# Jobs of the recurrence issued in three pieces, and a first stage whose modulation comes in four parts with other loads behind it

## The chip, the cores and the metric

The kernel runs on one core of one Trainium2 chip. The metric is the device time of one execution in microseconds (us). Five engines work side by side, each through its own list of instructions in order: PE (TensorE: matrix products and transposes), DVE (VectorE), ACT (ScalarE), POOL (GpSimd) and SP (SyncE, which here mostly issues transfers). In the profile, PE's weight loads stand under PEld. An instruction that depends on another engine waits for a semaphore, and everything behind it on its own engine waits with it.

## The reference

One layer for 512 noisy grid tokens and 128 context tokens (640 in all, width 1024):

```
sh1, sc1, g1, sh2, sc2, g2 = split(silu(cvec) @ w_ada + b_ada, 6)     # the modulation
h = rmsnorm(x, norm1_g) * (1 + sc1) + sh1
u_rw, u_na, gate_rw, gate_na = split(h @ w_in)
o_rw, state = rwkv(u_rw)           # forward and backward recurrence over time, 8 heads of 64
  # per step: sa = s @ a;  s = s * w + sa b^T + v k^T;  y = s @ r
  # bonus = sum(r * k_bonus * r_k) * v, added to the normalised y
o_na = neighbourhood or context attention (q, k normalised; v)
x = x + g1 * ((sigmoid(gate_rw) * (o_rw @ w_o_rwkv) + sigmoid(gate_na) * (o_na @ w_o_na)) @ w_out)
h2 = rmsnorm(x, norm2_g) * (1 + sc2) + sh2
x = x + g2 * ((silu(h2 @ ffn_w1) * (h2 @ ffn_w3)) @ ffn_w2)
```

The scan is computed in chunks, by a triangular inverse within each chunk.

## The kernel before, in words

**First stage (0 to 62 us).** Tokens stand in five blocks of 128 (four of the grid, one of context, loaded by `x_load`). `norm_x(i)` normalises a block and transposes it on PE (tile `xt`) into `xT`. The modulation's first two vectors are made in parts: `ada_part(k0, n, c0)` loads tiles `wa` of `w_ada` through SP and multiplies them with the conditioning vectors into `psa`, and `mod_part(k0, n, c0)` copies `psa` to `rows` (DVE), transposes `rows` on PE (`pc`), makes scale `A` and shift `B` on DVE, and then, for the n blocks of 128 columns of the width that begin at k0, makes `h` from `xT`: the high half on ACT, `ht` and the low half on DVE. Columns k0 = 0 and 1 are part one, 2 and 3 part two, 4 to 7 part three. The first user of `h` is the Q projection: `tok_gen` steps through four chunks of `w_qkv`, each loaded as `wst`, split into `whi` (ACT) and `wlo` (DVE), and multiplied in steps of three matmuls of 512 columns (`acc`): 40 steps, 120 matmuls, then K and V follow. The numbers in `qp` say how many steps of Q stand on PE behind each tile of `wa`. What SP loads for later stages (`win`, `upw`, `gup`, `f`) is put by the scheduler into its list where it fits.

**Recurrence (240 to 640 us).** It runs over four groups of heads (ct 0 to 3). For each, `inv` builds the inverse of a triangular matrix `RL` on DVE in 30 steps s of a product (`pr`) and a sum; on PE stand meanwhile independent matmuls of later or earlier projections, the fillers (`fl`, 128x320), whose number behind each step is written out in `plan`. Three jobs (`v_job`, `t_job`, `g_job`, on lines 8 to 15, 0 to 7 and so on of the chunk) are put into `inv` at the steps in `jobs`, (2, 9, 28) or (2, 8, 28): each of the second and third makes 192 records of 64x64 on PE in one go, 64 of `t_job` (L1274) and 128 of `g_job` (L1216, L1219, L1252 or L1263). The results' masks follow on DVE at the steps in `mds`. `bonus` sums over the heads with a constant matrix, in two halves: matmul (L1162), product on DVE (L1164), matmul, product, each at a step of its own; `g_job` reads the tile rows `R_`, `BK` and `vp`. After step 30 DVE transposes `RL` into `RT` (L1346), and PE goes on with the carry products from L1359 on.

In the first stage `manual_schedule` keeps PE's instructions in the written order; in the other engines' lists the scheduler places them. In the recurrence the generators of the stage and of the fillers are stepped by the tables, and that sets PE's and DVE's order.

## Time and profile before

| | us |
|---|---|
| median of 3 runs | 1145.75 (1142.03 to 1146.5) |
| profiled execution, its own time | 1141.53 |
| span of the profiled execution, first to last instruction | 1139.8 |
| PE busy in the span | 1106.1 |
| DVE busy | 781.1 |
| ACT busy | 533.7 |
| POOL busy | 193.7 |
| mean granted clock of PE | 0.997 |

PE is busy for 97% of the span, so an instruction that is moved there only matters through PE's idle time, some 34 us in all. The other engines are idle for much longer, and their idle time counts only where PE waits for them. The views below name, for a stretch or an engine, what it did and what ended its idle time; "issue" means that the engine waited for nothing the profile shows.

### The profile page before, as it was taken

How to read it: one execution, taken by the hardware profiler on the slowest of the kernel's cores; microseconds unless marked ns; L12 is line 12 of the kernel's file. 1: busy time of each engine (PE TensorE's matmuls, PEld its weight loads, DVE VectorE, ACT ScalarE, POOL GpSimd, SP SyncE). 2: the span in 40 equal slices, each digit the busy share in tenths (PEclk: the TensorE clock that was granted, in tenths of full speed). 3: DMA queues.
4: the chain of work that ended last, by engine and by line, in shares of the span. 5: the costliest groups of instructions: out<-in, count | busy, mean ns of one | idle time of the engine just before them, and what ended most of it. 6: DMA issues, size and time to landing. Idle time of an engine off the chain costs nothing.

```text
span 1139.8 us, 26864 instructions
## 1 busy us (share of the span) xinstructions
PE 1106.1 (97%) x11160; PEld 979.3 (86%) x11160; DVE 781.1 (69%) x1646; ACT 533.7 (47%) x1056; POOL 193.7 (17%) x261
## 2 busy tenths in 40 slices
PE   6999999999999999999899999999999999999998
PEld 4688878799888988888898788999899989998997
DVE  4565465769658948946777846996478647864776
ACT  4444566664574565566353525654134413441340
POOL 1163244320101211111100511200001010101000
PEclk9999999999999999999999999999999999999999
DMA  9752677654423443343734961223112321232122
GB/s 342 266 107 97 191 263 264 200 152 111 126 65 96 115 121 94 107 110 98 276 97 134 260 215 64 90 77 120 65 59 90 114 72 56 93 108 77 56 94 93
DMA packets 60482, 149.16 MB, mean 131 GB/s; under 512 B 7460, under 2 KB 22436, under 8 KB 60360
## 3 DMA queue, kind: packets, MB, share of 16 engines
q1 hardware_dynamic: 54312, 129.85, 35.0%
q0 software_dynamic: 4032, 14.68, 6.6%
q10 hardware_dynamic: 2016, 2.90, 0.8%
q8 instruction: 88, 1.44, 0.5%
q14 instruction: 34, 0.28, 0.1%
HBM read 118.41 MB, written 14.32 MB: 116 GB/s over the span
## 4 chain that ended last, share of the span: by engine, by line
PE 71%; DVE 11%; issue 7%; ACT 5%; DMA 5%; POOL 1%; SPq 0%; ACTq 0%; DVEq 0%; POOLq 0%
PE acc L311 23%; PE f L1880 21%; PE fl L223 9%; PE mm L223 4%; DMA wa<-in_w_ada_dram 2%; DVE RL L1333 1%; DVE pr L1329 1%; PE po L1011 1%; PE psa L1049 1%; PE pt L993 1%; PE lg L964 1%; DMA win<-in_rpbp_dram 1%; PE w L1449 1%; PE fl L587 1%; PE w L1462 1%
## 5 line engine op out<-in xcount | busy, mean ns | idle before, releaser
L1880 PE MATMUL f<-t,whi 128*128 128x320 f32 x640 | 141.7, 309 | 0.2
L311 PE MATMUL acc<-whi,u 128*128 128x512 f32 (+1 forms) x448 | 136.0, 385 | 0.0
L1880 PE MATMUL f<-b,whi 128*128 128x320 f32 x608 | 135.0, 310 | 0.4 <-DVE b L212 0.4
L223 PE MATMUL fl<-h,whi 128*128 128x320 f32 x672 | 121.6, 321 | 0.0
L1880 PEld LDWEIGHTS f<-t,whi 128*128 128x128 f32 x640 | 106.8, 188 | 0.8 <-issue 0.4
L223 PEld LDWEIGHTS fl<-h,whi 128*128 128x128 f32 x672 | 101.5, 188 | 4.9
L192 ACT CAST whi<-wst 128x1024 fp32r<-128x1024 f32 (+1 forms) x77 | 79.3, 1033 | 54.6 <-PE acc L311 28.3
L1880 PEld LDWEIGHTS f<-b,whi 128*128 128x128 f32 x608 | 101.7, 188 | 1.1 <-issue 0.6
L1880 PE MATMUL f<-t,wlo 128*128 128x320 f32 x320 | 98.9, 309 | 0.0
L311 PEld LDWEIGHTS acc<-whi,u 128*128 128x128 f32 x448 | 83.5, 188 | 16.6
L1880 PE MATMUL f<-b,wlo 128*128 128x320 f32 x304 | 94.0, 309 | 0.0
L1933 ACT CAST whi<-ws 128x1024 fp32r<-128x1024 f32 x40 | 42.0, 1051 | 104.5 <-PE f L1880 45.6
L311 PE MATMUL acc<-wlo,u 128*128 128x512 f32 (+1 forms) x224 | 86.3, 385 | 0.0
L1947 POOL TENSOR_TENSOR ws<-wst 128x512 f32<-128x512 f32 x20 | 28.9, 1447 | 334.9 <-DVE wlo L1936 226.3
L195 DVE TENSOR_TENSOR wlo<-wst,whi 128x1024 fp32r<-128x1024 f32 (+2 forms) x57 | 60.2, 1066 | 28.2 <-ACT whi L192 27.7
L311 PE MATMUL acc<-whi,h 128*128 128x512 f32 x240 | 78.5, 401 | 0.7 <-DVE h L436 0.7
L1748 DVE SCALAR_TENSOR_TENSOR tt<-acc,G 128x512 f32<-128x512 f32 (+1 forms) x51 | 34.7, 680 | 59.9 <-PE acc L311 44.6
L223 PE MATMUL fl<-h,wlo 128*128 128x320 f32 x336 | 63.3, 320 | 0.0
L1933 ACT CAST whi<-wst 128x1024 fp32r<-128x1024 f32 (+1 forms) x48 | 41.4, 870 | 42.3 <-PE acc L311 37.6
L191 POOL DMA_DIRECT2D wlo<-wst x28 | 24.8, 886 | 210.8 <-ACT wlo L190 194.9
L1880 PEld LDWEIGHTS f<-t,wlo 128*128 128x128 f32 x320 | 60.1, 188 | 0.0
L1936 DVE TENSOR_TENSOR wlo<-ws,whi 128x1024 fp32r<-128x1024 f32 x40 | 55.4, 1385 | 5.4 <-ACT whi L1933 5.4
(341 smaller groups left out, 2528.5 us busy)
## 6 DMA issues: line engine op xcount, KB each, us to landing
wst<-in_w_dram SPq DMA_DIRECT2D x66, 512.0 KB
wst<-in_w_rw_dram SPq DMA_DIRECT2D x31, 512.0 KB
wlo<-wst POOLq DMA_DIRECT2D x28, 512.0 KB, 4.8
wa<-in_w_ada_dram SPq DMA_DIRECT2D x24, 512.0 KB
f<-in_w_ada_dram SPq DMA_DIRECT2D x16, 512.0 KB
wst<-in_w_qkv_dram SPq DMA_DIRECT2D x12, 512.0 KB
o<-o_d SPq DMA_DIRECT2D x14, 320.0 KB
x<-in_xs_dram SPq DMA_DIRECT2D x8, 512.0 KB
```

Source lines behind the costliest of these rows:

```text
L191: pool.dma_start(lo[:, :n].bitcast(F32), st[:, :n], accum_op=ALU.add)
L192: act.copy(hi[:, :n], st[:, :n])
L195: dve.tensor_tensor(out=lo[:, a:b], in0=st[:, a:b], in1=hi[:, a:b].bitcast(F32), op=ALU.subtract)
L223: pe.matmul(ps[:, :t1 - t0], w[:, a:a + 128], x[:, k0 + kt, t0:t1], start=n == 0, stop=n == 3 * nk - 1)
L311: pe.matmul(pss[i][:, a:b], lhs(x, kt, ts_), w[:, cs_], start=ki == 0 and n == 0, stop=ki == last and n == 2)
L587: pe.matmul(ps[hf][:, :H2], u[:, kt * 128:kt * 128 + 128], x[:, kt, a:b], start=kt == 0 and n == 0, stop=kt == 7 and n == 2)
L964: pe.matmul(psl[:, hd, o_:o_ + n], qT[ft][rows, qs], x[rows, :], start=True, stop=True)
L1748: dve.scalar_tensor_tensor(out=tt, in0=ps[:, a:b], scalar=c, in1=G[:, g, sl], op0=ALU.mult, op1=ALU.mult)
L1880: pe.matmul(ps[:, :H2], w_[:, c_], x_[:, kt, :], start=first and kt + n == 0, stop=last and kt == 3 and n == 2, skip_group_check=more)
L1933: act.copy(r[0][:, :width], src())
L1936: dve.tensor_tensor(out=r[1][:, :width], in0=src(), in1=r[0][:, :width].bitcast(F32), op=ALU.subtract)
L1947: eng_x(PRM["se"][i - 1]).tensor_tensor(out=o_, in0=x, in1=y, op=op)
```

## The change

In the first stage the modulation is made in four parts of two column blocks each (k0 = 0, 2, 4, 6), so all 16 `wa` tiles are loaded as two halves of 256 columns (before: eight so, eight with 512 columns). `qp` is now one string for each part: `a` loads and multiplies one tile, a number stands for so many Q steps, `w` loads Q's second chunk, `x` and `n` load and normalise the fifth block of tokens, `m` begins the part's modulation, and `t` finishes what is begun. The first part's `h` is made for tokens 0 to 255, then 256 to 511, then the rest. `tok_gen` gets an explicit order of the first two chunks' steps (`steps`), in which the fifth block of tokens comes later. `pin` ties loads for later stages behind the last `wa` load.

In the recurrence `g_job` is a generator that stops after four lines; at steps 9 to 11 and 26 to 28 `inv` issues `t_job`, then four lines of `g_job`, then four more, with fillers between. `jobs` is (2, 9, 26) for each ct, and masks are at steps 4 and 14 (before 4 and 12). `bonus` issues both matmuls at one step and the two products at the next two steps. The fillers' table in `plan` is rearranged: its sums for each stage are the same, but the three entries behind the last steps are smaller (24, 20, 10 become 20, 18, 9 in ct 0), and those around the jobs take what they lose.

```diff
-    qp=((0, 0, 7, 6, 7), (2, 5, 4, 4, 3, 2, 5, 3, 1)), ada=2, pa=1, pd=0,
+    qp=("a a w 7 a x 3 a 2 m 12", "a 6 a 6 n a t 6 a 3 m 9", "t 6 a a 6 a 6 a 3 m t"), ada=2, pa=1, pd=0,
...
-    h2=0.91, jobs=((2, 9, 28), (2, 9, 28), (2, 9, 28), (2, 8, 28)),
-    mds=((4, 12), (4, 12), (4, 12), (4, 12)), bud=((1.8, 0.8), (1.3, 1.8)), off=6, tk=2, h3=1,
+    h2=0.91, jobs=((2, 9, 26),) * 4, mds=((4, 14),) * 4, bud=((1.8, 0.8), (1.3, 1.8)), off=6, tk=2, h3=1,
...
+            if steps and ci < len(steps):
+                order = steps[ci]
...
+    def pin(ins):
+        tc.add_manual_dep(ins.ins, urgent[-1].ins.name, mybir.DependencyInfo(
+            mybir.DependencyClass.NoSync, mybir.DependencyReason.DATA), reason="order")
...
-        for g, (a, b) in enumerate(((0, 512), (512, NT))):
-            if g:
-                yield
+        for (a, b) in groups:
+            yield
+            g = int(a >= 512)
...
+            q0.append(wload(w_qkv[0]))
+            g = ada_part(2, 2, 128)
+            next(g)
+            mod = mod_part(0, 2, 0, ((0, 256), (256, 512), (512, NT)))
+            next(mod)
             norm_x(3)
-            q0.append(wload(w_qkv[0]))
-            x_load(4)
-            mod = mod_part(0, 2, 0)
+            next(mod)
             next(mod)
...
-            for hf in range(2):
-                hs_ = slice(hf * H2, (hf + 1) * H2)
-                ps = wps()
-                pe.matmul(ps[:, :H2], kc("blk1", 128), S.bv[:, hs_], start=True, stop=True)
-                yield
-                dve.tensor_tensor(out=S.bv[:, hs_], in0=ps[:, :H2], in1=v[:, hs_], op=ALU.mult)
-                yield
+            hs_ = [slice(hf * H2, (hf + 1) * H2) for hf in range(2)]
+            ps = [wps() for _ in hs_]
+            for p_, h_ in zip(ps, hs_):
+                pe.matmul(p_[:, :H2], kc("blk1", 128), S.bv[:, h_], start=True, stop=True)
+            yield
+            for n, (p_, h_) in enumerate(zip(ps, hs_)):
+                if n:
+                    yield
+                dve.tensor_tensor(out=S.bv[:, h_], in0=p_[:, :H2], in1=v[:, h_], op=ALU.mult)
...
+                if l == l0 + 4:
+                    yield 0
...
+                if begun and next(begun[0], None) is None:
+                    begun.pop()
                 if s in jobs:
                     for f in (v_job, t_job):
                         f(S, *jobs[s])
-                    masks.append(g_job(S, *jobs[s]))
+                    g = g_job(S, *jobs[s], masks)
+                    if s < 5:
+                        drain(g)
+                    else:
+                        begun.append(g)
```

**SP, the loads from the fifth `wa` tile on.** Before (names: `wa` modulation weights, `wst` weights of Q and then K, `x` tokens; `win`, `upw`, `f` are for later stages):

```order
L174 DMA wst_251<-in_w_qkv_dram 128x1024
L384 DMA x_257<-in_xp_dram 128x1024
L392 DMA wa_284<-in_w_ada_dram 128x2x256 x2
L392 DMA wa_295<-in_w_ada_dram 128x2x256 x2
L392 DMA wa_306<-in_w_ada_dram 128x2x256 x2
```

```order
L174 DMA wst_429<-in_w_qkv_dram 128x1024
L863 DMA win_1024<-in_rpbp_dram 128x1x249
L863 DMA win_1027<-in_rpbp_dram 128x1x249
L392 DMA wa_440<-in_w_ada_dram 128x2x512
L615 DMA upw_1217<-in_lup_dram 128x512
L1030 DMA f_221_1297<-in_w_ada_dram 128x1024
L1030 DMA f_260_1486<-in_w_ada_dram 128x1024
L174 DMA wst_543<-in_w_qkv_dram 128x1024
```

The same places after:

```order
L173 DMA wst_232<-in_w_qkv_dram 128x1024
L399 DMA wa_238<-in_w_ada_dram 128x2x256 x2
L399 DMA wa_301<-in_w_ada_dram 128x2x256 x2
L399 DMA wa_312<-in_w_ada_dram 128x2x256 x2
L173 DMA wst_315<-in_w_qkv_dram 128x1024
L399 DMA wa_337<-in_w_ada_dram 128x2x256 x2
L385 DMA x_340<-in_xp_dram 128x1024
```

```order
L399 DMA wa_579<-in_w_ada_dram 128x2x256 x2
L173 DMA wst_635<-in_w_qkv_dram 128x1024
L891 DMA win_1080<-in_rpbp_dram 128x1x249
L891 DMA win_1083<-in_rpbp_dram 128x1x249
L643 DMA upw_1273<-in_lup_dram 128x512
L1058 DMA f_225_1353<-in_w_ada_dram 128x1024
L1058 DMA f_264_1542<-in_w_ada_dram 128x1024
```

The context block (`x_257`, now `x_340`) moves from before the fifth `wa` tile to behind the eighth, and `win`, `upw` and `f` move from among Q's loads to behind them.

**PE, the last of the first stage's `pc`.** Before, one matmul of Q stands between the last product into `psa` and the transpose `pc`:

```order
L261 MATMUL psa<-wa_478,cs 32x256 x4
L311 MATMUL acc_311<-whi_431,h_90 128x512
L419 MATMUL pc_490<-K,rows_488 128x128 x2
L311 MATMUL acc_311<-whi_431,h_94 128x512
L311 MATMUL acc_311<-wlo_432,h_90 128x512
```

After, the third part's `pc`, and so the fourth's (`psa<-wa_579`, `pc_595`):

```order
L260 MATMUL psa<-wa_474,cs 32x128 x8
L427 MATMUL pc_490<-K,rows_488 128x128
L312 MATMUL acc_318<-whi_387,h_90 128x512
L312 MATMUL acc_318<-whi_387,h_94 128x512
L312 MATMUL acc_318<-wlo_388,h_90 128x512
```

The transpose has moved to stand directly behind the products whose sum it transposes.

**PE, the end of `t_job` and the start of `g_job` in ct 2, second job.** Before:

```order
L1274 MATMUL w_6206<-K,f_833_5751 64x64
L1274 MATMUL w_6207<-K,f_833_5751 64x64
L1252 MATMUL w_6242<-K,vp_627 64x64 x2
L1216 MATMUL w_6243<-AG,f_833_5751 64x64 x2
L1219 MATMUL w_6244<-R__2901,f_833_5751 64x64
```

After:

```order
L1306 MATMUL w_6262<-K,f_837_5807 64x64
L1306 MATMUL w_6263<-K,f_837_5807 64x64
L222 MATMUL fl_6195<-h_95,whi_5925 128x320
L222 MATMUL fl_6195<-h_92,whi_5925 128x320
L222 MATMUL fl_6195<-h_96,whi_5925 128x320
L222 MATMUL fl_6195<-h_92,whi_5925 128x320
L1284 MATMUL w_6306<-K,vp_683 64x64 x2
L1248 MATMUL w_6307<-AG,f_837_5807 64x64 x2
L1251 MATMUL w_6308<-R__2957,f_837_5807 64x64
```

Four fillers now stand between `t_job` and `g_job`; five more stand after `g_job`'s fourth line.

## Rows read from the trace of the kernel before

**Rows 1.** The page, part 1: busy time, share of the span, instructions

```profile
PE 1106.1 (97%) x11160; PEld 979.3 (86%) x11160; DVE 781.1 (69%) x1646; ACT 533.7 (47%) x1056; POOL 193.7 (17%) x261
```

**Rows 2.** Stretches: length, busy PE, PEld, DVE, ACT, POOL; granted clock, DMA share, GB/s

```profile
0.00:20.00 20.00, 10.50 (x113) 7.01 (x113) 8.77 (x31) 10.59 (x18) 2.75 (x10) 1.00 0.96 330
20.00:45.00 25.00, 23.35 (x173) 13.20 (x174) 11.40 (x27) 7.22 (x11) 1.45 (x3) 0.93 0.98 351
...
256.00:288.00 32.00, 30.77 (x642) 29.24 (x642) 31.44 (x128) 13.94 (x30) 2.60 (x10) 1.00 0.45 115
348.50:385.00 36.50, 35.51 (x656) 33.28 (x654) 34.54 (x134) 19.39 (x39) 8.13 (x16) 1.00 0.39 102
439.40:478.00 38.60, 35.62 (x655) 33.26 (x654) 34.24 (x133) 19.17 (x37) 8.26 (x16) 1.00 0.35 99
537.80:579.00 41.20, 38.30 (x680) 36.52 (x679) 34.90 (x132) 17.54 (x35) 6.03 (x10) 1.00 0.67 222
```

**Rows 3.** Waits of PE, whole span: total us, times, longest

```profile
PE w L1219 <- issue: 2.5, 2, 1.3
...
PE w L1216 <- issue: 1.4, 1, 1.4
```

**Rows 4.** Timeline of PE, start of Q: start, duration, instruction, idle before

```profile
20.07 0.42 PE L261 MATMUL psa<-wa,cs 128*32 128x128 f32 x8 [0.34 <-DMA wa<-in_w_ada_dram]
20.82 0.42 PE L261 MATMUL psa<-wa,cs 128*32 128x128 f32 x8 [0.33 <-DMA wa<-in_w_ada_dram]
21.18 0.50 PE L311 MATMUL acc<-whi,h 128*128 128x512 f32 x1
22.42 0.50 PE L311 MATMUL acc<-whi,h 128*128 128x512 f32 x1 [0.74 <-DVE h L436]
```

**Rows 5.** The stretch with a lower granted clock (columns as in Rows 2)

```profile
23.00:26.80 3.80, 3.80 (x25) 3.01 (x27) 1.17 (x3) 0.36 (x1) 0.00 (x0) 0.55 1.06 390
```

**Rows 6.** Timeline of PEld, third part of the modulation

```profile
38.76 0.16 PEld L261 LDWEIGHTS psa<-wa,cs 128*32 128x32 f32 x8 [0.77 <-DMA wa<-in_w_ada_dram]
...
40.12 0.16 PEld L261 LDWEIGHTS psa<-wa,cs 128*32 128x32 f32 x8 [0.49 <-DMA wa<-in_w_ada_dram]
...
44.71 0.20 PEld L419 LDWEIGHTS pc<-K,rows 128*128 128x128 f32 x2 [0.43 <-DVE rows L416]
```

**Rows 7.** Timeline of PE, end of Q (its 120th product stands before 61.64)

```profile
61.41 0.39 PE L311 MATMUL acc<-wlo,h 128*128 128x512 f32 x1
61.64 0.61 PE L311 MATMUL acc<-whi,h 128*128 128x512 f32 x2
```

**Rows 8.** Second job of ct 0 and of ct 2 (columns as in Rows 2)

```profile
264.89:267.75 2.86, 2.86 (x193) 2.86 (x192) 2.72 (x13) 1.29 (x3) 0.00 (x0) 1.00 0.02 6
...
451.80:456.25 4.45, 3.24 (x193) 3.07 (x192) 4.26 (x25) 1.12 (x3) 2.16 (x3) 1.00 0.12 42
```

**Rows 9.** DMA queues, 453.2 to 453.3 us: packets, MB; then PE's restart

```profile
q8 instruction: 1, 0.02, 63.4%
```

```profile
455.56 0.27 PE L1219 MATMUL w<-R__2901,f 64*64 64x64 f32 x2 [1.21 <-issue]
```

**Rows 10.** Timeline of DVE: the two products of `bonus` in ct 2

```profile
448.15 0.49 DVE L1164 TENSOR_TENSOR bv<-w,vp 128x320 f32<-128x320 f32 x1 [1.39 <-PE w L1162]
...
451.31 0.49 DVE L1164 TENSOR_TENSOR bv<-w,vp 128x320 f32<-128x320 f32 x1 [2.09 <-PE w L1162]
```

**Rows 11.** Timeline of PE, second job of ct 3

```profile
552.74 0.28 PE L1219 MATMUL w<-R__2901,f 64*64 64x64 f32 x3 [1.63 <-DVE bv L1164]
```

**Rows 12.** Timelines of DVE, then PE: end of `inv` in ct 3

```profile
577.35 2.04 DVE L1346 STREAM_TRANSPOSE f<-RL 128x1024 f32<-128x1024 f32 x1
```

```profile
581.07 0.75 PE L223 MATMUL fl<-o,wlo 128*128 128x320 f32 x4
581.65 1.19 PE L223 MATMUL fl<-o,whi 128*128 128x320 f32 x7
582.77 0.45 PE L1359 MATMUL w<-f,Nt 32*32 32x32 f32 x15
```

More of the change, by code (lines that the diff above doesn't have):

```diff
@@ L451, in body @@
                 pass
+            q0.append(wload(w_qkv[0]))
[3 more added lines that the diff above has]
+            next(mod)
             norm_x(3)
-            q0.append(wload(w_qkv[0]))
-            x_load(4)
-            mod = mod_part(0, 2, 0)
+            next(mod)
             next(mod)
             psq = {}
-            qg = tok_gen(psq, pp, (hh, hl), q0 + [w_qkv[i] for i in range(1, 4)], list(range(8)), range(5))
+            four = list(range(4))
+            steps = ([(k, i) for k in (0, 1) for i in four],
+                     [(2, i) for i in four] + [(0, 4), (1, 4)] + [(3, i) for i in four] + [(2, 4), (3, 4)])
+            chunks = q0 + [lambda: wcast(q0[1])] + [w_qkv[i] for i in (2, 3)]
+            qg = tok_gen(psq, pp, (hh, hl), chunks, list(range(8)), range(5), steps=steps)
             derived()
@@ L464, in some_q @@
                     next(qg)
[L466 to L478 removed]
+            todo = [mod]
+            for k0, row in zip((2, 4, 6), PRM["qp"]):
+                for e in row.split():
+                    if e.isdigit():
+                        some_q(int(e))
+                    elif e == "a":
+                        next(g, None)
+                    elif e == "w":
+                        q0.append(wdma(w_qkv[1]))
+                    elif e == "x":
+                        x_load(4)
+                    elif e == "n":
+                        norm_x(4)
+                    elif e == "t":
+                        while todo:
+                            drain(todo.pop(0))
+                    elif e == "m":
+                        drain(g)
+                        mod = mod_part(k0, 2, 64 * k0, ((0, 512), (512, NT)))
+                        next(mod)
+                        next(mod)
+                        todo.append(mod)
+                        if k0 < 6:
+                            g = ada_part(k0 + 2, 2, 64 * k0 + 128)
             tc.keep_in_program_order(act.dma_start(K[:, 128:], consts[:, 128:KO["nam"]]))
@@ L614, in prep_dma @@
         S.upw = upw
-        eng.dma_start(upw[:, 0:512], lup[ct, :, 0:512])
         S.gup = kp.tile([P, 128], F32, tag="gup", bufs=2, name=nm("gup"))
-        eng.dma_start(S.gup, lup[ct, :, 512:640])
+        for dst, a, b in ((upw[:, 0:512], 0, 512), (S.gup, 512, 640)):
+            ins = eng.dma_start(dst, lup[ct, :, a:b])
+            if not ct:
+                pin(ins)
     def prep_cast(S):
```

60 lines of the change are left out of this document (25 added, 35 removed).

## The prediction

> **What bounds the kernel now.** I read the page first: PE is busy for 1106.1 of 1139.8 us [rows 1]. The change takes no product away, so it can only win from the 33.7 us in which PE idles and from stretches in which PE's clock is low, or lose by adding to either. Then the busy time by stretch, to see where the idle time lies: 9.5 us from 0 to 20, 1.65 us from 20 to 45, and 1.2, 1.0, 3.0 and 2.9 us in the four inverses that the change touches [rows 2]. The other 946 us hold 14.4 us of it. DVE is busy in the inverses for 31.4 of 32, 34.5 of 36.5, 34.2 of 38.6 and 34.9 of 41.2 us [rows 2]: ct 0 and 1 are bound by DVE, ct 2 and 3 by PE's list with its stalls. The table of PE's waits names the largest of these: 2.5 and 1.4 us of "issue" in front of the small matmuls of `g_job` [rows 3]. Last comes the clock: from 23.0 to 26.8 us the granted clock is 0.55 in the mean, that is, most of it is spent at the lower of the two levels (1.2 instead of 2.4 GHz) [rows 5]. It costs (1 - 0.55) x 3.80 = 1.7 us of PE's work.
>
> The sum is made against the profiled execution, 1141.53 us, which is the span and 1.7 us around it. The median of the runs shown, 1145.75, lies 4.2 us higher, and the runs differ by 4.5 us; the forecast is the sum set off from the median.
>
> **First stage: the start of Q.** Q's first product starts at 21.18, right behind a `wa` tile whose halves came at 20.07 and 20.82, PE waiting for each [rows 4]. So a half of 256 columns takes 0.75 us on the queue, while two tiles of 512 columns came 40.12 - 38.76 = 1.36 us apart [rows 6]. The context tokens, another load of 512 KB, move from before this tile to behind the eighth: the tile ends 1.36 us sooner, and Q begins at about 19.8. Gain 1.3 us. The second product waits 0.74 us for DVE's low half of `h` [rows 4]. With groups of 256 tokens that operation is half as long, but it begins no sooner relative to the loads; I leave the 0.7 us.
>
> **First stage: the loads behind.** `win`, `upw` and two tiles `f`, 1.53 MB or 4 us at 1.36 us per 512 KB, leave the middle of Q's loads; eight tiles in halves cost 2 x 0.75 - 1.36 = 0.14 us more each, 1.1 us. The later weights come up to 3 us sooner, but PE waited little for them: PEld 0.77 and 0.49 us [rows 6], PE itself some 0.5 in all, since products still ran. What the change adds stands on PE: two `pc` transposes lie directly behind their own `psa`, so DVE's copy to `rows` has no cover. With one product of 0.23 us [rows 7] in between, PEld waited 0.43 us there [rows 6]; without it the wait is 0.66. Two of them, less the old one, are 0.9 us. Behind a waiting `pc` all of Q's products are queued. Then tile `wa_337`: two tiles in halves and Q's second chunk, 2 x 1.5 + 1.36 = 4.4 us, lie between it and the tile of 20.82 - 1.36 = 19.5, so it is there at 23.9; PE, from a second product at 21.1, reaches it after nine products (9 x 0.23) and one `psa` (some 0.6) at 23.8. Wait 0 to 1.1, taken 0.4. In all -1.3 - 0.5 + 0.9 + 0.4 = -0.5, and 0.1 for more instructions: -0.4. The low clock at 23 us follows PE's idle time up to 22.4. If PE idles less, that stretch may go, worth up to 1.7; the waits that remain speak against it. Taken 0.9 on even odds. The first stage gives -1.3, with ends +0.7 and -3.4. It counts in full, as PE hardly waits behind it (14.4 us in 946).
>
> **Jobs in three pieces.** The second job of ct 0 runs its 192 records in 2.86 us without a gap; in ct 2 it takes 4.45 us, with PE busy for 3.24 [rows 8]. There PE stops for 1.21 us and waits for nothing that is shown; 2.3 us before its restart one 16-KB packet of instructions was moved [rows 9]. The same pattern stands behind the other stops, together the 3.9 us of "issue" [rows 3]. My reading: 192 records, each a weight load and a matmul, are 384 instructions in 2.86 us, which outruns the instructions' arrival when a block ends inside. Now 64 records (0.95 us) are followed by four to six fillers at 0.58 / 4 = 0.145 us each [rows 12], so the same instructions are spread over 0.6 to 0.9 us more per piece, and a stop of 1.3 us shrinks to some 0.6 or goes. But the place of the blocks in the list shifts too, and bursts that had no stop before (nine of twelve) may get one. Ends: 3.9 (all three go) and 0.7 (three halved, 1.9 saved, and two new ones of 0.6 come). I take 2.0, nearer to the half.
>
> The Trainium skill speaks against this reading ("Runtime: NRT & Kernel Launch", section "Instruction fetch mechanics"): it says that the sequencer fetches the next 16-KiB block while it works on the current one, so that crossing a block is mostly hidden. By that rule the stops have another cause and the pieces save nothing, and the sum is 2.0 us smaller. The rows, a packet 2.3 us before a restart, do not agree with it so far.
>
> **The bonus.** In ct 2 DVE sat idle for 1.39 and 2.09 us until the halves' matmuls came [rows 10]. Both matmuls now stand together, the second eight places earlier, and their products a step later, so that DVE does a step of the inverse meanwhile. That frees 3 us of DVE in ct 2, but PE's own idle time there, 3.0 us, bounds what reaches the end, and 2.6 us of it are the "issue" counted above. In ct 3 DVE's gain is idle anyway: PE reaches the carry at 582.77, and DVE's transpose ended at 579.39 [rows 12]. In ct 1 PE has 1.0 us of idle time in all. I take 0.8 for ct 1 and ct 2 together, between 0 and 2.
>
> The cost: `g_job`'s first line now needs a product that comes a step later. In ct 3 PE already waited 1.63 us for it [rows 11]; I expect 1.6 to 1.9 there, no change, with all the fillers queued behind. In ct 0 to 2 the fillers between the pieces (0.6 us) cover the step by which the product moved (some 0.65 us of DVE's time), and I take 0.
>
> **Fillers, masks, pins.** The sums of the fillers are unchanged. Three of them move in front of the carry's first matmul, 3 x 0.145 = 0.44 us in ct 0, 1 and 2. Where PE is late already this is the same work in another order; in ct 0 and 1 DVE's work behind the carry starts up to 0.44 us later, with other fillers on PE meanwhile. Cost 0 to 0.9, taken 0.3. The masks at step 14 have no user before the carry, and the pinned loads none before 62 us: nothing, and if a pinned `f` tile were late, its matmuls would hold K's products by at most the tile's 1.4 us.
>
> **The sum.** -1.3 (first stage) - 2.0 (pieces) - 0.8 (bonus) + 0.3 (fillers) = -3.8 us: 1137.7 for the profiled execution, 1142.0 from the median.
>
> **Rivals.**
> 1. *All of it works.* The three stops go (3.9), the bonus gives 2.0, the low clock goes (1.7) and Q starts 1.3 sooner, less 0.2 of moved fillers: -8.7, so 1137.0. For it: the stops are the largest idle item inside the inverses, and the low clock directly follows an idle time that shrinks. Against it: ct 3 keeps its wait for the bonus product, and DVE in ct 2 is busy for 34.2 of 38.6 us.
> 2. *The pieces spread the stops* (the slower side). If 64 records already outrun the instructions' arrival, the eight second and third jobs stop once each, not three of them. Eight stops of 1.3 us are 10.4 instead of 3.9; with 0.4 won in the first stage the time is 1145.75 + 6.5 - 0.4 = 1151.9. It is a loss from four stops on. Against it: with fillers between, the mean rate over a block is lower than now.
> 3. *Nothing changes in the recurrence.* "Issue" has a cause that pieces do not touch, or as many stops remain, and DVE's order sets the rest. Only the start of Q is left, -0.4, and the low clock stays: 1145.3. The Trainium skill's section named above would have it so.
>
> **How the numbers follow.** About 0.5% of the time, 5.7 us, is what a measurement of this kernel can tell from no change. The forecast gets 0.42 (1142.0, from 1139 to 1144.5), rival 1 0.30 (1137.0, from 1134 to 1139.5), rival 3 0.18 (1145.3), rival 2 0.10 (1151.9, from 1148 to 1154). Faster by over 0.5%, under 1140.0: rival 1 and the edge of the forecast, 0.32. Slower, over 1151.5: most of rival 2, 0.08. The rest, 0.60, is within 0.5%. The range leaves out the lower part of rival 1 and rival 2: 1135.5 to 1148.
>
> **What would show it.** In the trace after: Q's first product at 19.8 +- 0.4 and its last about 1.3 us sooner than before [rows 7]; two waits of 0.5 to 0.7 us on `pc` for `rows`; a low clock at 23 us or none. In the inverses: "issue" in front of the small matmuls under 2.5 us in all where it was 3.9; DVE without the two waits in ct 2; in ct 3 a wait of 1.6 to 1.9 us of `g_job`'s first line for the second bonus product. I am wrong if "issue" is 3.5 us or more, if PE waits for the bonus product in ct 0 to 2, if what PE gains in an inverse comes back as a wait of the carry, or if a `wa` tile comes more than 1.1 us after PE is ready for it.

## The result, and the profile after

The changed kernel takes 1149.5 us (median of 11 runs, 1146.69 to 1151.7) where the kernel before takes 1143.05 (11 runs on the same chip): a ratio of 1.0047, with a 95% interval of 1.0036 to 1.0057. By that ratio it is slower by 5.4 us (the medians differ by 6.45). The prediction, 1142.0 with a range to 1148.0, had the sign wrong, and the time lies outside the range. Its base, the median of three runs, 1145.75, was 2.7 us above the median of these eleven; as a difference it forecast -3.8 us and +5.4 came. The profiled execution took 1148.02 us, with a span of 1146.2.

The page of the kernel after, part 1 (busy time, share of the span, instructions), against [rows 1]:

```profile
PE 1109.0 (97%) x11224; PEld 978.4 (85%) x11224; DVE 782.4 (68%) x1656; ACT 534.5 (47%) x1058; POOL 193.7 (17%) x261
```

PE makes 64 matmul records more (32 products more into `psa`, two records each) and is busy for 2.9 us longer, and the span is 6.4 us longer. To see where, I compare the times at which the two traces pass the same places. Minus is a lead of the kernel after:

| place | before, us | after - before, us |
|---|---|---|
| Q's first product | 21.18 | -0.53 |
| Q's end (start of K's first product) | 61.64 | -1.65 |
| V's end (start of its last product) | 120.57 | -1.59 |
| DVE reaches the recurrence's first transpose | 255.56 | +1.77 |
| carry of ct 0 begins (L1359 before) | 287.76 | +4.94 |
| carry of ct 1 | 385.17 | +4.24 |
| carry of ct 2 | 479.12 | +5.25 |
| carry of ct 3 | 582.77 | +6.48 |
| end of the span | 1139.75 | +6.49 |

So there are three parts: 1.6 us won in the first stage, 3.4 us lost between V and the recurrence, in work that the change does not touch, and 4.7 us lost in the recurrence. From 583 us on nothing happens.

The first stage. Timeline of PE after (start, duration, instruction, idle before), for [rows 4], and below it the stretch of [rows 5]:

```profile
19.30 1.42 PE L260 MATMUL psa<-wa,cs 128*32 128x128 f32 x32
20.65 0.49 PE L312 MATMUL acc<-whi,h 128*128 128x512 f32 x1
21.53 0.50 PE L312 MATMUL acc<-whi,h 128*128 128x512 f32 x1 [0.39 <-DVE h L444]
```

```profile
23.00:26.80 3.80, 3.80 (x43) 2.43 (x43) 2.30 (x9) 1.68 (x2) 0.00 (x0) 1.00 1.05 359
```

Q starts 0.53 us sooner and not 1.4. Before, PE waited for the halves of the tile [rows 4]; now it waits for DVE's `rows` instead, and behind that the end of `xt` and the same 32 records of `psa` run without a gap:

```profile
17.87 0.33 PE L427 MATMUL pc<-K,rows 128*128 128x128 f32 x1 [1.48 <-DVE rows L424]
```

The stretch at the lower clock is gone: granted 1.00 where it was 0.55.

Waits of PE after, whole span (total us, times, longest):

```profile
PE psa L260 <- DMA wa<-in_w_ada_dram: 6.5, 2, 6.1
PE pc L427 <- DVE rows L424: 2.3, 3, 1.5
...
PE fl L222 <- ACT fl L621: 2.1, 1, 2.1
PE pt L1021 <- POOL L L1015: 2.1, 5, 0.8
...
PE w L1175 <- ACT pre L1170: 1.7, 1, 1.7
PE fl L222 <- issue: 1.6, 2, 1.0
...
PE w L1306 <- issue: 1.2, 1, 1.2
...
PE w L1295 <- issue: 0.9, 1, 0.9
```

"Issue" has 3.7 us in the last three of these lines, against 3.9 in [rows 3]: four stops, behind the records at 258.50, 283.50, 443.29 and 542.84 us, for three. (A fourth of before, 0.6 us at 254.87, just ahead of the recurrence, is gone.) The second of the four, 0.92 us, stands inside a piece, the last of ct 0's third job. Two waits for ACT are new, 1.7 and 2.1 us. The wait for the bonus product of [rows 11] is gone.

The pieces are where the listing of the change put them. Timeline of PE after, second job of ct 0; `L1306` is `t_job`, `L1284` the first matmul of a line of `g_job`:

```profile
266.62 1.16 PE L1306 MATMUL w<-K,f 64*64 64x64 f32 x64
267.71 0.86 PE L222 MATMUL fl<-h,whi 128*128 128x320 f32 x4
268.50 0.27 PE L1284 MATMUL w<-K,vp 64*64 64x64 f32 x2
...
269.59 0.99 PE L222 MATMUL fl<-h,whi 128*128 128x320 f32 x5
270.51 0.27 PE L1284 MATMUL w<-K,vp 64*64 64x64 f32 x2
...
271.60 0.42 PE L222 MATMUL fl<-h,whi 128*128 128x320 f32 x1
```

From the first of 64 records to the filler behind them it is 1.09 us, three times, 3.27 in all. In the kernel before, 192 records in a row take 2.86 us [rows 8], 2.96 to the filler behind them.

### The profile page after: what moved, and what is told of

The parts are those of the page before. It is cut to its first block, busy times and chain, and to the rows that moved or that the text cites. A ratio compares the mean times of both kernels' runs of the same rounds, so it can differ in the third digit from the quotient of the medians.

```text
span 1146.2 us, 27010 instructions
## 1 busy us (share of the span) xinstructions
PE 1109.0 (97%) x11224; PEld 978.4 (85%) x11224; DVE 782.4 (68%) x1656; ACT 534.5 (47%) x1058; POOL 193.7 (17%) x261
## 4 chain that ended last, share of the span: by engine, by line
PE 76%; DVE 7%; issue 7%; ACT 6%; DMA 3%; POOL 1%; SPq 0%; DVEq 0%; ACTq 0%; POOLq 0%
PE acc L312 24%; PE f L1918 21%; PE fl L222 12%; PE mm L222 4%; DMA o_d<-on 1%; PE lg L992 1%; PE pt L1021 1%; PE po L1039 1%; PE psa L1077 1%; ACT whi L191 1%; PE w L1487 1%; PE w L1306 1%; PE w L1251 1%; DMA o<-o_d 1%; ACT wlo L189 1%
## 5 line engine op out<-in xcount | busy, mean ns | idle before, releaser
L312 PE MATMUL acc<-whi,u 128*128 128x512 f32 (+1 forms) x448 | 135.9, 385 | 0.0
L1918 PE MATMUL f<-b,whi 128*128 128x320 f32 x608 | 135.0, 310 | 0.4 <-DVE b L211 0.4
L222 PE MATMUL fl<-h,whi 128*128 128x320 f32 x672 | 124.2, 322 | 1.0 <-issue 1.0
```

What stands on the lines that cost most here:

```text
L222: pe.matmul(ps[:, :t1 - t0], w[:, a:a + 128], x[:, k0 + kt, t0:t1], start=n == 0, stop=n == 3 * nk - 1)
L312: pe.matmul(pss[i][:, a:b], lhs(x, kt, ts_), w[:, cs_], start=ki == 0 and n == 0, stop=ki == last and n == 2)
L1918: pe.matmul(ps[:, :H2], w_[:, c_], x_[:, kt, :], start=first and kt + n == 0, stop=last and kt == 3 and n == 2, skip_group_check=more)
```

## The experiments

The question was which part of the change costs what, and why stops come and go in code that the change leaves alone. First the two halves apart, the recurrence without the pieces, and a shift of PE's list alone.

**a_first** has the changed first stage and `pin`, and before's recurrence.

> The first stage of the changed kernel (four parts, pinned loads, explicit order) with the recurrence of before. In the trace of the changed kernel Q ends 1.65 us sooner, V ends 1.59 us sooner, but the recurrence begins 1.77 us later: 3.4 us are lost in the attention stage. Theory one (the loads of the first stage bring the later transfers into another rhythm, and the attention stage waits for them): V ends 1.6 us sooner, the recurrence begins 1 to 2 us later than before, total +1 to +2.5 us. Rival (the loss in attention was particular to that execution): the 1.6 us stay to the end, total -1 to -2 us. In both the three stops named issue inside the inverses of ct 2 and 3 may move, which is worth up to 1.4 us each, because the first stage has 128 more instructions on PE, half a 16-KB block.

Measured: 1151.74 against 1143.01, 1.0070 (1.0051 to 1.0090), far over the +1 to +2.5 us expected. V ends 0.89 us sooner, and yet the kernel is no faster than with the whole change. Most of the loss stands in the recurrence, which is before's word for word: 9.3 us from the first transpose to ct 3's carry. Timeline of PE in ct 0, jobs that ran without a stop in the kernel before:

```profile
259.73 0.34 PE L1303 MATMUL w<-K,f 64*64 64x64 f32 x7 [1.13 <-issue]
270.08 0.27 PE L1245 MATMUL w<-AG,f 64*64 64x64 f32 x2 [0.90 <-issue]
285.86 0.27 PE L1245 MATMUL w<-AG,f 64*64 64x64 f32 x1 [3.21 <-issue]
```

```profile
q8 instruction: 1, 0.02, 28.0%
```

The last row is the DMA queue from 283.4 to 283.6 us: a packet of instructions 2.4 us before the restart at 285.86, as in [rows 9]. Behind that stop the clock falls as well. The stretch in a_first (columns as in [rows 2]), and the only one of its kind in the recurrence of the kernel before:

```profile
286.50:289.90 3.40, 3.40 (x14) 3.40 (x14) 3.33 (x6) 1.46 (x3) 0.00 (x0) 0.52 0.47 159
```

```profile
299.60:303.10 3.50, 3.50 (x26) 3.05 (x26) 0.30 (x2) 3.41 (x8) 0.87 (x1) 0.51 0.39 151
```

The trace of a_first has three such stretches of some 3.4 us at the lower clock, from 286.7, 310.6 and 587.0 us, the first and the last right behind stops of 3.2 and 2.1 us. The kernel after has none. So a part of the 9.3 us, which this trace does not separate, is the clock's.

**b_rec** has the changed recurrence and before's first stage. **b_joined** is b_rec with the eight lines of `g_job` in one go again:

```diff
-                    if s < 5:
-                        drain(g)
-                    else:
-                        begun.append(g)
+                    drain(g)
```

> The first stage of before with the recurrence of the changed kernel (jobs in three pieces, both bonus matmuls together, new filler table). Theory one (each break in a run of 64x64 records costs PE 0.22 us, since a filler follows a record after 0.148 us and a record follows a filler after 0.238 us where records follow each other after 0.015; 16 new breaks are 3.6 us, and as many stops for instructions remain as before): total +3.5 to +5 us, PE busy in each inverse about 1.2 us longer. Rival (the loss of the changed kernel comes from its first stage, and the recurrence only starts later): total -1 to +1 us.

> As the kernel with the first stage of before and the new recurrence, but each job is issued whole at its first step (9 or 26), so that no filler stands inside a run; the filler table, the steps of the masks and the bonus stay new. Theory one (the breaks cost 0.22 us each): 3 to 4 us faster than the pieced one, so within 1.5 us of before. Rival (the new filler table or the bonus costs the time): no more than 1 us faster than the pieced one.

Measured: b_rec 1145.36, 1.0020 (1.0009 to 1.0031); b_joined 1146.3, 1.0030 (1.0019 to 1.0041). In b_rec no job behind the first one stops; PE's "issue" in the recurrence is the first line below. In b_joined two stops of 1.1 and 1.0 us are back, in the lines under it:

```profile
PE w L1195 <- issue: 0.7, 1, 0.7
```

```profile
PE w L1222 <- issue: 1.1, 1, 1.1
PE w L1219 <- issue: 1.0, 1, 1.0
PE w L1195 <- issue: 0.7, 1, 0.7
```

At this shift the pieces do take the stops away, and it does not make the recurrence faster: it is 331.9 us long in b_rec, 330.4 in b_joined and 327.2 before. That b_joined would be 3 to 4 us faster than b_rec was a miss: without a single break it is no faster by its runs. Its trace has the stops back, 2.1 us, and keeps the two new waits for ACT (1.5 and 2.1 us), so these do not come from the breaks but from the new steps of the jobs and the fillers' table.

**s32a** is the kernel before with 32 products of 64x64 more in the first stage. Each is two weight loads and two matmuls, so PE's list grows by 128 instructions, as by the changed first stage.

```diff
+            zp = pp.tile([P, 512], F32, tag="tp", name=nm("zp"))
+            for _ in range(32):
+                pe.matmul(zp[0:64, 0:64], ident[0:64, 0:64], ident[0:64, 0:64], start=True, stop=True)
```

> The kernel before with 32 small matmuls more in the first stage, in a place where PE waits for loads; they add 128 instructions to PE's list, half a 16-KB block, and 0 to 1 us. Theory one (the stops named issue stand where a block of 256 instructions ends inside a run of records): the stops of 1.2 to 1.4 us at the second job of ct 2, the third of ct 2 and the second of ct 3 vanish or shrink, others may come in bursts that had none; the total changes by -3 to +3 us. Rival (the stops have a cause at those places, for instance a wait that the trace does not show): the three stops stay where they are.

Measured: 1160.4, 1.0153 (1.0132 to 1.0174). The stops are those of a_first. In the trace 6.0 us of its loss come at 642 to 722 us, where the scheduler had moved a late load of weights (below); of the rest, 3.1 us come between V and the recurrence and 6.0 in the recurrence. Timeline of PE, for the third of a_first's:

```profile
287.34 0.21 PE L1219 MATMUL w<-AG,f 64*64 64x64 f32 x1 [3.48 <-issue]
```

**The rule in the places.** I counted PE's instructions (weight loads, matmuls, semaphores) from the start of each trace. Every stop inside a job, of every kernel, stands at a count of 193 in each 256. The page shows 88 packets of instructions for 22448 weight loads and matmuls, 255 to a packet: so I read the place of a stop as the end of a block. But most ends make none. A job of 192 records is a burst of 384 instructions. Over eight kernels, an end that lay 0 to 279 instructions into such a burst made no stop, and an end 301 or more into it always one of 0.9 to 3.7 us (an end at 297 made none). An end shortly behind a burst, among the fillers, can make one too: a_s48 has stops of 0.8 and 3.3 us there. In the kernel before, three of the eight bursts have an end at 302 to 313: those of ct 2 and the second of ct 3. A shift by 128 takes them out and puts others in.

The Trainium skill ("Runtime: NRT & Kernel Launch", section "Instruction fetch mechanics") says that the next 16-KiB block is fetched while the current one runs, so that a crossing is mostly hidden. The trace agrees for most of the 88 blocks; for an end late in a burst it does not, and there the measurement decides.

If that is right, a shift by 256 must bring the stops back to before's places, and any other must move them. **after_s32** and **a_s32** are the changed kernel and a_first with the 32 products of s32a (128 + 128 = 256), **a_s48** is a_first with 48 (a shift of 320, that is 64), **s64a** is the kernel before with 64 (256).

> The changed kernel with 32 small matmuls more in its first stage, while PE waits for loads: 128 instructions, so that PE's list of the recurrence stands again as before against the blocks of 256 (the first stage of the change alone adds 128). Theory one (the change's first stage moved the ends of the blocks into other places; the stops at 258.5, 283.5, 443.3 and 542.8 us, 4.7 us, and what the attention stage loses, 3.4 us, come from that): these stops go, the time falls by 4 to 8 us against the changed kernel, to within 2 us of the kernel with the old first stage and the new recurrence. Rival (the loads of the new first stage cost the time, and the added matmuls change nothing): no change against the changed kernel, or 1 us more.

> The first stage of the change with the recurrence of before, and 32 small matmuls more in the first stage: 256 instructions more than before in all, one whole block. Theory one: the stops stand where they stood before (ct 2 and ct 3, 4.5 us in all), the 3.4 us of ct 0 go, and the time is before minus the 0.9 to 1.6 us that the first stage wins, less up to 0.5 us for the matmuls: -1.5 to 0 us against before, some 9 us less than without the 32 matmuls. Rival (the loads): 7 to 9 us above before, as without them.

> As the kernel with the first stage of the change, the recurrence of before and 32 matmuls more, but with 48: one block and 64 instructions. Theory one: the stops move again, by 64 instructions against the program; in every stop PE has executed a number of instructions that leaves the same rest, 193, when divided by 256, and an instruction packet began 2.2 to 2.5 us before PE goes on. The total lies anywhere between before and 8 us above. Rival: as with 32.

> The kernel before with 64 small matmuls more in the first stage, 256 instructions, one whole block: the control for the kernel with 32. Theory one (it is the place of the blocks, not the added work): the recurrence runs as before, with the three stops of before, and the large stops of the kernel with 32 (3.7 us in ct 0, 2.2 in ct 3) are gone; between the end of V and the carry of ct 3 no more than 1 us is lost against before. Rival (the added matmuls, or the order that the scheduler finds with them, cost the time): at least as slow in the recurrence as with 32, 8 to 9 us.

Measured: after_s32 1146.12, 1.0017 (1.0008 to 1.0026); a_s32 1148.9, 1.0041 (1.0029 to 1.0053); a_s48 1151.36, 1.0063 (1.0051 to 1.0075); s64a 1150.17, 1.0061 (1.0046 to 1.0076). The stops went where the count says: in a_s32 and s64a to the three of before, in a_s48 to 272.75, 286.06, 357.70 (a small one, 0.2 us) and 584.65 us. The times were another matter, for two reasons that have nothing to do with the stops. The added products delay Q by 2.0 to 5.7 us. And in a_s32, s64a and s32a the scheduler moved a late load: PE waits 3.3 to 3.7 us for it, and behind the wait the granted clock is 0.50 for some 7 us, together 5.7 to 6.3 us at 642 to 722 us. In a_s32, the wait and then the stretch:

```profile
PE acc L313 <- DMA wlo<-wst: 3.7, 1, 3.7
```

```profile
674.00:680.00 6.00, 5.49 (x13) 4.33 (x14) 1.21 (x2) 0.00 (x0) 0.00 (x0) 0.50 0.75 212
```

So I read these kernels by the length of the recurrence (table below). after_s32 is free of the second fault: the same change with its blocks back in place is slower by 0.17% and not by 0.47%, although it starts Q 2.5 us late.

**b_bonus** is the kernel before with the new `bonus` and its steps alone; **b_pieces** is the rest of the changed recurrence (pieces, `jobs`, `mds`, fillers) with the old `bonus`.

> The kernel before with the bonus of the change alone: both matmuls at one step, the two products at later steps, and the filler table's third column that steps them; jobs, masks and fillers as before. Theory one (the two new waits of the changed kernel in ct 2 and ct 3, 1.7 us for ACT's pre and 2.1 us for ACT's fl, come from the moved jobs and fillers): neither wait appears, DVE's two waits in ct 2 (3.5 us) shrink to under 1, the stops for instructions stay at their places, since the number of PE's instructions is the same: total -1.5 to 0 us. Rival (the bonus brings the new waits): they appear, total +1.5 to +4 us.

> The kernel before with the jobs of the change alone: three pieces with fillers between, jobs at 2, 9, 26, masks at 4 and 14, and the filler numbers of the change; bonus and its steps as before. Theory one (the moved jobs and fillers bring ACT's new waits, and 16 breaks of 0.22 us cost PE 3.6 us while the three stops, 3.9 us of idle time, go): total +2 to +4 us, as with all of the new recurrence, with both waits for ACT in it. Rival (the bonus brings the waits): total -1 to +1 us, no wait of PE for ACT's pre or fl over 1 us.

Measured: b_bonus 1144.14, 1.0006 (0.9993 to 1.0020); b_pieces 1146.39, 1.0029 (1.0018 to 1.0040). The bonus is worth nothing. It takes away the wait of [rows 11], and in its place PE waits in ct 3 for ACT:

```profile
PE w L1213 <- ACT TG L1271: 1.7, 1, 1.7
```

In b_pieces no job after the first one stops, and it is still slower by 0.29%.

**a_s32b** is a_s32 with its 32 products a little further on, behind the first tile of `wa`, which leaves the late load alone. **a_s32c** has them behind Q.

> The first stage of the change with the recurrence of before, and 32 small matmuls at the very start of PE's list, where PE waits 5 us for the first weights; again one whole block of 256 instructions more than before. Theory one (with the blocks back in place the new first stage keeps what it wins, if nothing else moves): Q starts at 20.7, not 23.7 as with the matmuls later in the stage; the three stops of before stand at their places; the transfers behind the recurrence are issued as in the kernel without the matmuls, so its wait of 3.7 us for a weight's low half does not come; total -1.5 to 0 us against before. Rival (the first stage loses its gain in the attention stage in any case): total 0 to +2 us.

> The changed first stage alone, with 32 products of 64x64 more on PE behind the last product of Q, where they delay nothing of the first stage (a_s32b had them at its start, and lost there what the stage wins). Together with the 32 more products into psa that is one whole block of 256 PE instructions, from there on. They change no result. Theory (place of the blocks): Q ends 1.4 to 1.9 us earlier than before; behind it the dummies cost about 0.5 us (192 such products took 2.86 us); from then on PE's blocks end where they did before, so the attention stage loses at most 0.8 us, the stops stand in the second jobs of ct 2 and ct 3 as in before (three of 1.3 to 2.0 us) and the recurrence is as long as before's within 1.2 us: ratio 0.998 to 1.000. Rival (the first stage's moved loads cost the attention stage 2.5 to 3.4 us whatever the blocks do): the lead at V's end is gone by the recurrence's first DVE transpose, ratio 1.001 to 1.003. Rival (neither): stops as in the kernel with the changed first stage alone, 1.007.

Measured: a_s32b 1146.44, 1.0027 (1.0013 to 1.0041); a_s32c 1145.85, 1.0026 (1.0016 to 1.0037). In both the recurrence is as long as before's, 327.2 us. But a_s32b starts Q 2.4 us late, and in a_s32c the products cost far more than the 0.5 us that I had expected:

```profile
60.05 3.94 PE L512 MATMUL zp<-K 64*64 64x64 f32 x64
```

All of them go to one quarter of PE's array and into one output, 62 ns a record; a job's records use all four quarters in turn, 15 ns a record. Without these 3.9 us a_s32c would stand near 0.999, by my estimate.

**s7 and a_s39: a shift chosen ahead.** If the places alone decide, seven products more (28 instructions) behind Q must take the three stops out of the kernel before, since they put the ends at 302 to 313 down to 274 to 285 and raise no other into the bad part. **s7** is that, on all four quarters:

```diff
+            zp = [pp.tile([P, 512], F32, tag="tp", name=nm("zp")) for _ in range(2)]
+            for zi in range(7):
+                za, zb = zi & 1, zi >> 1 & 1
+                pe.matmul(zp[za][64 * zb:64 * zb + 64, 64 * (zi // 4 % 8):64 * (zi // 4 % 8) + 64],
+                          ident[64 * za:64 * za + 64, 0:64], ident[64 * za:64 * za + 64, 0:64], start=True, stop=True)
```

**a_s39** is a_first with 39 of them, which with its own 128 instructions is the same shift plus one block.

> The kernel before with seven 64x64 products more on PE behind Q, that is 28 instructions; they change no result. In the runs so far a block end of PE's list that falls 301 to 384 instructions into an unbroken burst of 384 always stopped PE for 0.9 to 3.7 us, one that falls 0 to 278 into it never. In before the bursts of ct 2 (two) and ct 3 (one) have it at 302 to 313. Seven products more put these ends at 274 to 285, and no other of the eight bursts gets one beyond 278. Theory (place of the blocks): no stop for issue over 0.5 us in any second or third job of the four inverses, where before had three of 1.43, 1.61 and 1.49 us; of these 4.5 us some 1 to 2 come back as waits that were hidden by them: 1140 to 1142 where before has 1143.4, ratio 0.997 to 0.999. Rival (the stops have to do with where the jobs lie in time, or with which job it is): the three stops stay where they are, ratio 1.000 to 1.001.

> The changed first stage (128 PE instructions more) with before's recurrence and 39 products more behind Q (156 instructions), so that PE's blocks end where they do in s7. The products go to all four quarters of the array in turn, so they should take 0.6 us in all; in a_s32c, where all 32 went to one quarter, they took 3.94 us (60.05 to 63.92), more than the whole ratio of that run. They change no result. Theory: no stop over 0.5 us in any second or third job, Q's end 1.2 to 1.9 us sooner less nothing, V's end 0.6 to 1.3 sooner, attention as in before within 1 us: ratio 0.996 to 0.999. Rival (moved loads cost the attention stage what the first stage wins): the lead at V's end is gone by the first DVE transpose of the inverse, and the ratio is that of s7 to 0.001. Rival (places of blocks don't decide): a stop of 3.4 us near 282 us as with the first stage alone, ratio 1.005 to 1.008.

Measured: **s7 1141.23, 0.9983 (0.9972 to 0.9995); a_s39 1140.89, 0.9976 (0.9963 to 0.9988).** Both are faster than the kernel before, by 0.2% with intervals that leave out 1, and neither computes anything less. The largest "issue" of PE in the recurrence, s7 and then a_s39:

```profile
PE w L1224 <- issue: 0.7, 1, 0.7
...
PE fl L223 <- issue: 0.7, 1, 0.7
...
PE w L1378 <- issue: 0.5, 1, 0.5
```

```profile
PE w L1407 <- issue: 0.7, 1, 0.7
```

One of the three stops is left in s7, 0.95 us from record to record in the second job of ct 2, at 286 instructions into the burst, one beyond where I had put it; a_s39 has that end at 285, and no stop. So "none over 0.5 us" was missed by one in s7, and the bad part has no sharp edge: 286 stopped here, 297 did not in b_joined. The second job of ct 2 in a_s39, for the second of [rows 8] (length, busy PE, PEld, DVE, ACT, POOL; clock, DMA share, GB/s):

```profile
453.31:456.27 2.96, 2.96 (x194) 2.89 (x193) 2.96 (x20) 1.09 (x3) 2.15 (x3) 1.00 0.00 0
```

2.96 us without a gap, where the kernel before needs 4.49 to the same place. Some 2 us are given back in ct 0: in s7 PE waits for `R_` there for 2.0 us, 1.2 before, and a stop of 0.97 us lies among fillers at 285.97. The granted clock is no part of their lead in the recurrence: each has one stretch at the lower level there, from 261 us, as the kernel before has one. Of a_s39's lead from the first stage the 39 products take 1.39 us, and V ends where it did before.

All lengths, from one trace each (shift: PE instructions more than before, modulo 256; low: stretches of some 3.4 us with a granted clock of 0.50, the lower level, in the recurrence):

| kernel | shift | V's end to recurrence, us | recurrence to ct 3's carry, us | low | ratio |
|---|---|---|---|---|---|
| before | 0 | 135.0 | 327.2 | 1 | 1 |
| after | 128 | 138.4 | 331.9 | 0 | 1.0047 |
| a_first | 128 | 137.5 | 336.5 | 3 | 1.0070 |
| s32a | 128 | 138.1 | 333.2 | 1 | 1.0153 |
| a_s48 | 64 | 136.0 | 331.4 | 2 | 1.0063 |
| after_s32 | 0 | 135.5 | 330.3 | 1 | 1.0017 |
| a_s32 | 0 | 135.8 | 326.5 | 1 | 1.0041 |
| s64a | 0 | 134.7 | 327.0 | 0 | 1.0061 |
| a_s32b | 0 | 134.5 | 327.2 | 1 | 1.0027 |
| a_s32c | 0 | 135.9 | 327.2 | 1 | 1.0026 |
| b_rec | 0 | 134.7 | 331.9 | 2 | 1.0020 |
| b_joined | 0 | 135.2 | 330.4 | 0 | 1.0030 |
| b_pieces | 0 | 134.9 | 331.2 | 1 | 1.0029 |
| b_bonus | 0 | 136.0 | 328.8 | 1 | 1.0006 |
| s7 | 28 | 135.6 | 325.9 | 1 | 0.9983 |
| a_s39 | 28 | 135.9 | 325.5 | 1 | 0.9976 |

Before's recurrence (a_first, s32a, a_s48, a_s32, s64a, a_s32b, a_s32c, s7, a_s39) goes with the shift, whichever first stage stands ahead of it: 326.5 to 327.2 us at 0, 325.5 and 325.9 at 28, 331.4 at 64, 333.2 and 336.5 at 128. A stretch at the lower clock halves PE's speed for 3.4 us, so it can cost up to 1.7 us; in the kernel before it costs 0.5 (against s64a, which has none, PE falls behind by 0.5 us from 297 to 306 us). The order by shift holds where the number of stretches is the same: one each at 0 (before, a_s32, a_s32b, a_s32c), 28 (s7, a_s39) and 128 (s32a). The change's recurrence is 330.3 to 331.9 us long at shifts 0 and 128, so at these two places the pieces make it nearly insensitive to the shift, at a price above that of the stops.

## Why the prediction was wrong, step by step

**First stage, -1.3: the size held, its make-up did not, and that is partly luck.** It won 1.65 us by Q's end. Of the 1.3 us for Q's start only 0.53 came, because the first `pc` waited 1.48 us for `rows`, a wait that the sum did not have. In this pair of traces the low clock that went makes up the difference: 0.53 + 1.7, less 0.6 of other waits. But that the change takes it away is not shown. b_bonus, with before's first stage and as much idle time ahead (PE busy for 2.97 of the 5 us from 18 to 23; before 3.11), has no such stretch either, and Q ends no sooner in it, since PE then waits for a tile of `wa`:

```profile
23.00:26.80 3.80, 3.80 (x35) 2.98 (x34) 1.97 (x6) 1.36 (x3) 0.00 (x0) 1.00 1.06 392
```

b_bonus waits 2.1 us for that tile at 39.2 us; the changed stage waits for no tile at this point. Two waits of `pc` were to be 0.5 to 0.7 us; the last two measured 0.41 each. No `wa` tile of the second half came late.

**"It counts in full, as PE hardly waits behind it": failed.** From V's end to the recurrence the kernel after lost 3.4 us. PE's waits for `L` there grew from 0.6 to 2.1 us and its busy time from 133.7 to 135.4. I had reasoned from the idle time of before, as if code that is not touched takes as long as before. The loss is not due to the loads that the change moves: s32a, with before's first stage, loses 3.1 there, and a_s39, with the changed one and another shift, 0.9. The traces show how the shift gets there. PE's `L` comes from POOL, which follows DVE and ACT, and ACT's next `on` waits for the store of the last one. Waits of ACT from 200 to 245 us, before and after:

```profile
ACT on L211 <- DMA o_d<-on: 2.3, 1, 2.3
```

```profile
ACT on L210 <- DMA o_d<-on: 4.6, 1, 4.6
```

It is 3.9 us in a_first, 5.3 in s32a, and 2.0 to 3.3 in the other kernels that have this wait. In SP's list the store stands behind loads, of which one takes longer to issue. Timelines of SP, before and after:

```profile
214.26 0.38 SPq L1030 DMA_DIRECT2D f<-in_w_ada_dram  x1
```

```profile
213.83 1.42 SPq L1058 DMA_DIRECT2D f<-in_w_ada_dram  x1
```

This issue takes 1.42, 1.11 and 1.61 us in the three traces with a shift of 128 and 0.38 in the thirteen others, and only in these three does a packet of PE's instructions begin within 0.4 us of it; in the others it is at least 2.6 us away. From 229 to 238 us PE loses 1.4 to 2.8 us by this chain. It is read from traces, no kernel tests it, and elsewhere most issues with a packet as near take their usual time, so that the meeting alone does not explain it. The other 1.0 to 1.2 us of after and a_first are lost by 168 us; their cause stays open.

**Pieces, -2.0: the mechanism was right, the sum lacked two terms.** The stops stand at the ends of blocks of PE's list, and in b_rec and b_pieces the pieces remove those inside the second and third jobs; in the kernel after one piece still has one. Three things went against the sum:

1. *The shift.* The prediction saw that "the place of the blocks in the list shifts too", and allowed two new stops of 0.6 us in the second and third jobs. It did not ask what 128 instructions more in the first stage do to all bursts behind, the first jobs and the fillers among them. The kernel after has stops of 1.15, 0.92, 0.95 and 0.63 us, 3.7 in all where it was 3.9: hardly anything saved, and over the 3.5 us that the prediction had named as the sign of being wrong. Rival 2 had one stop in each of eight jobs; there were four, one of them inside such a job.
2. *The breaks, counted at nothing.* A record follows a record after 0.015 us (the mean of 64) and a filler a filler after 0.147, but a filler follows a record after 0.148 and a record a filler after 0.238 (medians of the trace after). A job cut in three has two breaks more, each (0.148 - 0.015) + (0.238 - 0.147) = 0.22 us. Eight jobs are 16 breaks, 3.6 us; from the timeline above, 3.27 - 2.96 + 2 x 0.09 = 0.49 a job, 3.9 in all. That is PE's own time.
3. *Waits for ACT.* The prediction had none. The moved jobs and fillers changed ACT's list in ct 2. Timelines of ACT, before and after:

```profile
458.87 0.72 ACT L1142 COPY pre<-r 128x640 f32<-128x640 f32 x1
459.49 1.06 ACT L190 ACTIVATE wlo<-wst 128x1024 fp32r<-128x1024 f32 x1
460.45 1.04 ACT L192 CAST whi<-wst 128x1024 fp32r<-128x1024 f32 x1
```

```profile
463.77 1.05 ACT L189 ACTIVATE wlo<-wst 128x1024 fp32r<-128x1024 f32 x1
464.72 1.03 ACT L191 CAST whi<-wst 128x1024 fp32r<-128x1024 f32 x1
465.65 0.72 ACT L1170 COPY pre<-r 128x640 f32<-128x640 f32 x1
```

The copy `pre` now stands behind two casts of 2 us, and PE waits for it. In ct 3 ACT's order is as before, and it is PE's that changed: the fillers now stand ahead of the second job, which covered for them before (549.74 to 556.0 us), and PE waits for a filler's activation that stands behind an operation waiting 4.34 us for DVE (4.20 before). Timeline of PE, both:

```profile
466.43 0.77 PE L1175 MATMUL w<-K,pre 128*128 128x128 f32 x5 [1.71 <-ACT pre L1170]
...
558.09 0.70 PE L222 MATMUL fl<-o,whi 128*128 128x320 f32 x3 [2.14 <-ACT fl L621]
```

Both waits stand in b_rec too, with 1.72 and 2.14 us, in b_pieces and in b_joined, and neither in the kernel before or in b_bonus, so they come with the jobs and fillers.

**Bonus, -0.8: nothing.** DVE's two idle times in ct 2 did go, and in ct 3 the wait for the product too, where I had expected it to stay. But b_bonus is at 1.0006: what PE does not wait for in one place it waits for in the next (ACT's `TG`, 1.7 us, for the bonus product's 1.6).

**Fillers, +0.3: not told apart.** What the moved fillers cost the carry lies within the 4.7 us.

In sum: -1.6 (first stage) + 3.4 (up to the recurrence) + 4.7 (recurrence) = +6.5 in the traces. For the 4.7 there are 3.6 of breaks and 3.85 of ACT, less 1.6 of the bonus wait and 0.2 of "issue": 5.65. By groups of heads, up to the carry of each:

| ct | after - before, us | these terms, us |
|---|---|---|
| 0 | +3.17 | stops 2.07, breaks 0.9 |
| 1 | -0.70 | breaks 0.9 |
| 2 | +1.01 | ACT 1.71, breaks 0.9, "issue" 2.60 to 0.95 |
| 3 | +1.23 | ACT 2.14, breaks 0.9, "issue" 1.27 to 0.63, bonus wait -1.63 |

The sums come out within half a microsecond except in ct 1. There the kernel before waits 0.9 us for `Rt` and has its stretch at the lower clock, the kernel after neither; what each is worth is not separated. By runs, the shift's part of the 5.4 us is about 1.0047 - 1.0017, 3.4 us, although after_s32 starts Q late.

## What to carry to other kernels

When a stall that the profile calls "issue" ends some 2.4 us after the start of a packet of instructions, count the instructions: where the end of a block falls inside a burst of short instructions, or shortly behind it, decides the stall, and any edit ahead of it, however far, moves it. So cost an added instruction by what it does to the places behind it, compare versions at the same place of the blocks before judging an edit, and move the list by a few cheap instructions before spreading the burst out: seven idle products won the 2 us that the pieces were to win. Where an edit moves work, read the order of all engines, not of the bound one alone. And before a difference of 1 or 2 us between two traces is put down to an edit, set the stretches at the lower clock beside each other.

## What the runs showed of the hardware that I had not expected

- 128 instructions more on PE in the first stage made unchanged code 200 us later 9.3 us longer in a_first and 6.0 in s32a (327.2 to 336.5 and 333.2; a part of a_first's is its two stretches more at the lower clock), and 28 more made it 1.3 us shorter (s7).
- One stop can be 3.2 to 3.5 us of "issue" (a_first, s32a, a_s48), though the packet comes 2.4 us before the restart in a_first; most stops at other places are 0.6 to 2.1 us. Behind each of these three the granted clock falls to 0.50 for some 3.4 us.
- In three traces an issue of SP took 1.1 to 1.6 us instead of 0.38 beside a packet of PE's instructions, and the store behind it made ACT wait 1.6 to 3.0 us longer.
- Changing between records of 64x64 and products of 128x320 costs 0.22 us of PE for each pair of changes.
- Small products into one output on one quarter of the array take 62 ns a record (a_s32c), and on four quarters in turn 15 ns in a job and 18 in a_s39 (1.39 us for 78). Quarter and output were not told apart.
- From 23 to 26.8 us the granted clock was 0.55 in the kernel before, with PE busy for 3.11 of the 5 us ahead, and 1.00 in b_bonus with 2.97: the same idle time did not bring it down each time.
